# Store queue, rounding order and gated additions in a one-core decoder layer on Trainium2

## The chip, the cores and the metric

The kernel runs on one core of a Trainium2 chip. The core has five engines that the trace shows: TensorE (PE, with its weight loads as PEld), VectorE (DVE), ScalarE (ACT), GpSimd (POOL) and SyncE (SP). Each takes the instructions of its own list in order. SP, ACT and POOL can also issue DMA transfers; the trace shows these as SPq, ACTq and POOLq. The metric is the device time of one execution in microseconds (us); less is better.

## What is computed

The reference is one layer of a decoder trunk for two request groups that share weights: a prompt of 1024 tokens and 8 samples of 8 tokens. The kernel treats them as 1088 columns (NT). Cut to what matters here:

```
h = adaLN(RMSNorm(x), c);  P = h @ w_in
A = rwkv7_branch(P);  B = pool_branch(P)
x = x + gt * ((sigmoid(gA) * (A @ w_br_rwkv) + sigmoid(gB) * (B @ w_br_pool)) @ w_out)
h = adaLN(RMSNorm(x), c)
x = x + gt * (square(relu(h @ w_ff1)) @ w_ff2)      # 1024 -> 4096 -> 1024
y = RMSNorm(x)
```

Everything is float32. The change touches only the MLP, that is, the last three lines, and what stands directly around them.

## The kernel before

**Layout.** Features lie on the 128 partitions, tokens along the free dimension. x is eight tiles of 128 x 1088 (`self.xr[m]`), the hidden layer 32 blocks of 128 rows. A float32 product is made as three matmuls of rounded parts: each operand is split into `hi` (ScalarE's copy to the rounded type) and `lo` (VectorE's or GpSimd's difference), and hi*hi, hi*lo and lo*hi are summed in PSUM. For weights that is `halves` (L193 the rounding, L194 the difference, tiles `whi` and `wlo`); for the MLP's input combinations it is `parts` (L1397 the rounding, L1398 the difference).

**Seven products in place of eight.** Both MLP products are done by a 2x2 scheme with seven block products (numbers c = 0 to 6). For ff1 the halves are the two halves of the tokens (HF = 544 columns each) and the two halves of the 1024 input features; a pair j of hidden blocks is one unit, and there are 16 pairs. `norm2(0)` makes combinations 0 and 1 from the first token half. `norm2(1)` makes combination 5 and then, at L1445, combinations 6, 4, 2 and 3, each of four tiles k. A product of one combination with one weight block is 24 matmuls of 272 columns (`product`), into one of three PSUM tiles `pr`.

**Early pairs.** Products 0 and 1 of the first eight pairs (NE = 8) need only the first token half and run while `norm2(1)` is at work. They are ordered two pairs at a time: (0 of j, 0 of j+1, 1 of j, 1 of j+1). Product 1 is added on top of product 0 in the same PSUM tile, after ScalarE has copied product 0 out (`S["u"]`, L1530); when both are in, ScalarE copies the sum out (`S["o"]`, L1532). Both copies are stored to DRAM (`d_u`, L1533 and L1534) and read back later (L1492, L1493). Then all 16 pairs run, the early ones with products 5, 6, 4, 2, 3, the others with 0, 5, 1, 6, 4, 2, 3. VectorE adds and subtracts the products (L1546, L1548, L1553, L1554, L1558, L1566), ScalarE takes relu and square (L1514, L1515).

**Hidden blocks in DRAM.** For pairs 0 to 11 the combinations that ff2 needs are stored to DRAM: `d_ch` from `combos` (L1597, L1599), from L1573 and L1575, and from `apart` (L1584 for the early pairs, whose tile is a result of ScalarE; L1588 and L1589 for pairs 8 to 11, where ScalarE's rounding and VectorE's difference are stored apart). Pairs 12 to 15 are stored whole (`d_hid`, L1561 and L1569).

**ff2.** Three groups of pairs go through the seven products into accumulators ACC (L1699). `whole` then adds these to x with the gate: `a4 - x` (L1750) where needed, and `residual` (L1882 for the prompt columns, L1885 and L1887 for the sample columns). After ff2's sums, `second` runs `ff2_jobs(6)`: eight jobs, one for each block row m of x, in plain form, whose PSUM tiles (`mm`, `w`) are emptied by `residual` (L1882 again, with `hx<-mm,aq,hx`). After them follow the last group and the final norm.

**Order.** Only TensorE's order is the written one (`manual_schedule` for PE). For the other engines and queues a planner chooses at build time which ready instruction comes next on each list, by its own estimate of time, with the written order as priority; a dependency is the only way to hold an instruction back. The written order itself comes from generators that `Pace` interleaves: a `yield lambda: ...` waits until something has been written, a `yield 1500` until the estimated time has passed. `self.done` holds marks such as `("out", m, i)`.

**Lines that the prediction uses.** L1481 is the load of a raw weight block on SP (two slots `wraw`, four `wr`); L1495, L1497, L1498 and L1508 combine raw blocks; L1596 and L1598 are the first operations of `combos`; L1363 and L1364 are loads that ScalarE issues earlier in the program; L1860 stores the output.

## Time and profile before

| | |
|---|---|
| three runs | 1680.22, 1682.35 (median), 1683.54 us |
| profiled execution, its own time | 1684.85 us |
| its span, first to last instruction | 1683.1 us |
| mean granted TensorE clock | 0.982 |
| moved by DMA | 279.41 MB in 129474 packets |
| first product of the early pairs begins | 950.77 us |
| ff2's sums end, `ff2_jobs(6)` begins | about 1563 us |

How to read it: times in rows of the profile are us from the span's start. A row of a timeline gives start, length, engine, source line, operation, and `out<-in` tiles with shapes; x3 means three merged into one row. A bracket at the end gives the idle time of the engine just before the row and the operation that ended it. A row of a wait view reads "who waited <- for whom: us in total, times, longest us"; an SPq row is a wait at the head of SP's DMA queue. Rows for a source line give shortest/median/longest in ns and the first and last start in us.

### The profile page before, as it was taken

The page shows a single profiled execution, that of the slowest core. Times are in us where ns is not written, and L with a number is a line of the kernel's source. Part 1 is how long each engine was busy: PE and PEld are TensorE (multiplying, and loading weights), DVE is VectorE, ACT ScalarE, POOL GpSimd, SP SyncE. Part 2 cuts the span into 40 slices and gives each one's busy share as a digit, 9 for nine tenths or more (in the row PEclk, how much of TensorE's full clock was granted, in tenths as well). Part 3 has the DMA queues.
Part 4 walks back from the last instruction along what each step waited for, and adds up shares of the span by engine and source line. Part 5 has one row for each costly group of instructions (what it writes and reads, how often), then busy time and mean ns, then how long its engine had stood idle before and what let it go on. Part 6 is the DMA issues. An engine that isn't in the chain of part 4 may idle for free. (4 is left out here: it accounts for less than half of the span.)

```text
span 1683.1 us, 35182 instructions
## 1 busy us (share of the span) xinstructions
PE 1615.6 (96%) x14331; PEld 1503.0 (89%) x14331; DVE 1018.9 (61%) x1677; ACT 680.5 (40%) x1270; POOL 356.3 (21%) x392
## 2 busy tenths in 40 slices
PE   6999999999999999999999999899999999999897
PEld 3989878887888789879989999899999999999897
DVE  5686556845674456334546587675755577667746
ACT  4543333344334333412234464444555554323123
POOL 3311110010000000001622324453322131311221
PEclk9999999999998999999999999999999999999999
DMA  9333413232423242375984467666565876573112
GB/s 337 98 115 130 142 54 120 100 103 70 126 91 102 70 145 85 133 282 188 334 288 158 139 205 238 209 228 229 200 205 191 323 233 209 173 268 122 44 44 107
DMA packets 129474, 279.41 MB, mean 166 GB/s; under 512 B 16768, under 2 KB 31104, under 8 KB 129312
## 3 DMA queue, kind: packets, MB, share of 16 engines
q1 hardware_dynamic: 121632, 255.26, 44.7%
q10 hardware_dynamic: 6048, 16.23, 2.9%
q0 software_dynamic: 1632, 5.67, 1.0%
q8 instruction: 113, 1.85, 0.5%
q14 instruction: 49, 0.40, 0.1%
HBM read 198.15 MB, written 78.95 MB: 165 GB/s over the span
## 5 line engine op out<-in xcount | busy, mean ns | idle before, releaser
L170 PE MATMUL mm<-hx,whi 128*128 128x362 f32 (+1 forms) x1920 | 513.2, 349 | 5.7 <-ACT px L583 1.6
L170 PEld LDWEIGHTS mm<-hx,whi 128*128 128x128 f32 x1920 | 338.4, 193 | 42.4 <-issue 19.0
L170 PE MATMUL pr<-mr,whi 128*128 128x272 f32 x1792 | 340.3, 289 | 8.1 <-DVE hx L1566 6.0
L170 PE MATMUL mm<-hx,wlo 128*128 128x362 f32 (+1 forms) x960 | 318.5, 332 | 0.0
L170 PEld LDWEIGHTS pr<-mr,whi 128*128 128x128 f32 x1792 | 282.9, 190 | 12.0 <-issue 11.9
L170 PE MATMUL pr<-mr,wlo 128*128 128x272 f32 x896 | 259.2, 289 | 0.0
L193 ACT ACTIVATE whi<-wraw 128x512 fp32r<-128x512 f32 x201 | 126.3, 629 | 274.0 <-PE mm L170 83.0
L170 PEld LDWEIGHTS mm<-hx,wlo 128*128 128x128 f32 x960 | 185.0, 193 | 0.0
L194 DVE TENSOR_TENSOR wlo<-wraw,whi 128x512 fp32r<-128x512 f32 x146 | 109.1, 748 | 110.7 <-ACT whi L193 110.5
L170 PE MATMUL pr<-hx,whi 128*128 128x272 f32 x896 | 170.4, 289 | 4.1 <-ACT hid L1530 3.3
L170 PEld LDWEIGHTS pr<-mr,wlo 128*128 128x128 f32 x896 | 170.0, 190 | 0.0
L170 PE MATMUL mm<-mr,whi 128*128 128x272 f32 (+4 forms) x736 | 154.3, 304 | 4.1 <-DVE hx L1882 3.6
L170 PEld LDWEIGHTS pr<-hx,whi 128*128 128x128 f32 x896 | 141.5, 190 | 6.4 <-ACT hid L1530 3.7
L194 POOL TENSOR_TENSOR wlo<-wraw,whi 128x512 fp32r<-128x512 f32 x55 | 80.3, 1461 | 287.7 <-ACT whi L193 277.7
L193 ACT ACTIVATE whi<-wr 128x512 fp32r<-128x512 f32 x123 | 76.4, 627 | 143.8 <-PE pr L170 116.6
L170 PEld LDWEIGHTS mm<-mr,whi 128*128 128x128 f32 x736 | 119.8, 189 | 12.1 <-issue 7.8
L170 PE MATMUL pr<-hx,wlo 128*128 128x272 f32 x448 | 129.6, 289 | 0.0
L170 PE MATMUL mm<-mr,wlo 128*128 128x272 f32 (+4 forms) x368 | 110.7, 301 | 0.0
L194 DVE TENSOR_TENSOR wlo<-wr,whi 128x512 fp32r<-128x512 f32 x94 | 72.7, 774 | 31.3 <-ACT whi L193 31.3
L170 PEld LDWEIGHTS pr<-hx,wlo 128*128 128x128 f32 x448 | 85.0, 190 | 0.0
L170 PE MATMUL pr<-t,whi 128*128 128x272 f32 x448 | 84.4, 287 | 0.0
L1699 DVE TENSOR_TENSOR hx<-hx,pr 128x544 f32<-128x544 f32 x68 | 48.7, 716 | 42.4 <-PE pr L170 42.1
(381 smaller groups left out, 2637.3 us busy)
## 6 DMA issues: line engine op xcount, KB each, us to landing
wr<-in_w_ff SPq DMA_DIRECT2D x123, 256.0 KB, 3.4
wraw<-in_w_ff SPq DMA_DIRECT2D x85, 256.0 KB, 3.1
hid<-d_ch SPq DMA_DIRECT2D x72, 272.0 KB, 4.4
wraw<-in_w_in SPq DMA_DIRECT2D x68, 256.0 KB, 3.0
d_ch<-hx SPq DMA_DIRECT2D x52, 272.0 KB, 3.5
hid<-in_w_ada_mlp SPq DMA_DIRECT2D x24, 512.0 KB, 5.7
d_th<-px SPq DMA_DIRECT2D x22, 544.0 KB, 3.0
wt<-d_x SPq DMA_DIRECT2D x20, 544.0 KB, 4.2
```

Source lines behind the costliest of these rows:

```text
L170: return self.nc.tensor.matmul(out, lhsT, rhs, **kw)
L193: nc.scalar.activation(hi, raw, AF.Copy)
L194: (nc.gpsimd if pool else nc.vector).tensor_tensor(lo, raw, hi.bitcast(F32), op=ALU.subtract)
L1699: nc.vector.tensor_tensor(acc, acc, v, op=ALU.add)
```

## The change

There are three edits.

1. **Stores.** The transfers whose data ScalarE itself wrote last are issued from ScalarE's queue in place of SP's: both `d_u` stores, both `d_hid` stores, `apart`'s store for the early pairs (three a pair) and the `hi` store for pairs 8 to 11 (three a pair). The stores of VectorE's and GpSimd's results stay on SP.
2. **Roundings.** In `norm2(1)` combination 4 is written only after pair 5's second early copy, combination 2 only after pair 7's first. So that the planner keeps this order, the four roundings of each take their scale from a column `one`, which ScalarE fills twice: with a column of that copy, which makes it wait, and then with the constant 1. The column is `g2[:, c, 0:1]`, the prompt's scale, whose last use is before.
3. **Gated additions.** `whole` writes one block row m at a time, after job m-1 of `ff2_jobs(6)` has been written. Row m's gate (`gt[:, m, :]`) and a column -1 (`g2[:, m, 0:1]`) are first filled with a column of row m-1 of x (for m = 0 of the last accumulator), then with their values; the subtraction `a4 - x` becomes `x * (-1) + a4` with that column.

`pair_steps` returns its tile table as "S" for edit 2, and `ff2_jobs` marks ("six", m) for edit 3.

```diff
@@ -1392,9 +1392,9 @@
 
         C = {}
 
-        def parts(c, k, src, pool=False):
+        def parts(c, k, src, pool=False, one=1.0):
             hi, lo = C[c, k] = self.pair(self.hx, "hx", 16) if c < 2 else self.pair(p, "t", 4) if c == 3 else MR()
-            nc.scalar.activation(hi, src, AF.Copy)
+            nc.scalar.activation(hi, src, AF.Copy, scale=one)
             (nc.gpsimd if pool else nc.vector).tensor_tensor(lo, src, hi.bitcast(F32), op=ALU.subtract)
 
         def norm2(i):
@@ -1443,13 +1443,20 @@
             if i:
                 self.done.add(("C", 5))
                 for c in (6, 4, 2, 3):
+                    one = 1.0
+                    if c in (4, 2):
+                        j, h = (NE - 3, 1) if c == 4 else (NE - 1, 0)
+                        yield lambda: ("early", j, h) in self.done
+                        one = g2[:, c, 0:1]
+                        nc.scalar.activation(one, early[j]["S"]["o" if h else "u"][:, 0:1], AF.Copy)
+                        nc.scalar.activation(one, self.kc("one0")[:, 0:1], AF.Copy)
                     for k in range(4):
                         b21 = self.xr[k + 4][:, :HF]
                         if c == 6:
                             nc.vector.tensor_tensor(x[k], x[k + 4], x[k], op=ALU.subtract)
                         elif c == 3:
                             nc.vector.tensor_tensor(b21, tw[k], b21, op=ALU.subtract)
-                        parts(c, k, {6: x[k], 4: self.xr[k][:, :HF], 2: x[k + 4], 3: b21}[c])
+                        parts(c, k, {6: x[k], 4: self.xr[k][:, :HF], 2: x[k + 4], 3: b21}[c], one=one)
                     self.done.add(("C", c))
                     yield 1500
             self.done.add(("h2", i))
@@ -1530,11 +1537,13 @@
                             nc.scalar.activation(v2(S["u"]), v, AF.Copy)
                         elif early:
                             nc.scalar.activation(v2(S["o"]), v, AF.Copy)
-                            nc.sync.dma_start(self.d_u[0][j], S["u"])
-                            nc.sync.dma_start(self.d_u[1][j], S["o"])
+                            nc.scalar.dma_start(self.d_u[0][j], S["u"])
+                            nc.scalar.dma_start(self.d_u[1][j], S["o"])
                         else:
                             nc.scalar.activation(v2(S["o"]), v, AF.Relu)
                             nc.scalar.activation(S["o"], S["o"], AF.Square)
+                        if early == 1:
+                            self.done.add(("early", j, c))
                         return
                     ps = self.ps2()
                     yield from product(ps, c, w, True, True)
@@ -1558,7 +1567,7 @@
                         nc.vector.tensor_tensor(v2(o[:, HF:]), v2(S["u"]), v, op=ALU.add)
                         relu2(o[:, HF:])
                         if kept:
-                            nc.sync.dma_start(self.d_hid[j - 4 * NG], o)
+                            nc.scalar.dma_start(self.d_hid[j - 4 * NG], o)
                         else:
                             combos()
                     else:
@@ -1566,7 +1575,7 @@
                         nc.vector.tensor_tensor(v2(o[:, :HF]), v2(S["u1"]), v, op=ALU.subtract)
                         relu2(o[:, :HF])
                         if kept:
-                            nc.sync.dma_start(self.d_hid[4 + j - 4 * NG], o)
+                            nc.scalar.dma_start(self.d_hid[4 + j - 4 * NG], o)
                         else:
                             b21, b22, t2 = o[:, :HF], o[:, HF:], S["u1"]
                             nc.vector.tensor_tensor(t2, b22, S["u"], op=ALU.subtract)
@@ -1581,11 +1590,11 @@
             def apart(c, x, hi):
 
                 if early:
-                    nc.sync.dma_start(self.d_ch[c][j], x)
+                    nc.scalar.dma_start(self.d_ch[c][j], x)
                     return
                 nc.scalar.activation(hi.bitcast(F32R), x, AF.Copy)
                 nc.vector.tensor_tensor(x.bitcast(F32R), x, hi, op=ALU.subtract)
-                nc.sync.dma_start(self.d_ch[c][j], hi)
+                nc.scalar.dma_start(self.d_ch[c][j], hi)
                 nc.sync.dma_start(self.d_cl[c][j], x)
 
             def combos():
@@ -1599,7 +1608,7 @@
                 nc.sync.dma_start(self.d_ch[6][j], b12)
                 apart(0, b11, S.get("h0"))
 
-            return {c: (prep(c), run(c), c, j) for c in range(7)}
+            return {**{c: (prep(c), run(c), c, j) for c in range(7)}, "S": S}
 
         self.nr = 0
         early, steps = [pair_steps(j, 1) for j in range(NE)], []
@@ -1737,19 +1746,22 @@
         def whole():
 
             yield lambda: "sums" in self.done
-            gq = gt
-            nc.vector.tensor_copy(gq[:, 0, 0:1], ACC[3][1][1][:, 0:1])
-            nc.vector.tensor_copy(gq, self.aq[:, 16:24, :])
-            for mp in range(4):
-                (a1, a4), (a2, a3) = ACC[mp]
+            for m in range(8):
+                if m:
+                    yield lambda: ("six", m - 1) in self.done
+                (a1, a4), (a2, a3) = ACC[m // 2]
+                last = self.xr[m - 1] if m else ACC[3][1][1]
+                one, gate = g2[:, m, 0:1], gt[:, m, :]
+                for x in (one, gate[:, 0:1]):
+                    nc.vector.tensor_copy(x, last[:, 0:1])
+                nc.vector.memset(one, -1.0)
+                nc.vector.tensor_copy(gate, self.aq[:, 16 + m, :])
                 for i, s in enumerate(split):
                     c0, n = s.start, s.stop - s.start
-                    for h in range(2):
-                        x = (a1, a3)[h] if i == 0 else (a2, a4)[h]
-                        if h != i:
-                            nc.vector.tensor_tensor(x, a4, x, op=ALU.subtract)
-                        self.residual(self.xr[2 * mp + h], gq[:, 2 * mp + h, :])(c0, n, x)
-                yield 1500
+                    x = (a1, a3)[m % 2] if i == 0 else (a2, a4)[m % 2]
+                    if m % 2 != i:
+                        nc.vector.scalar_tensor_tensor(x, x, one, a4, op0=ALU.mult, op1=ALU.add)
+                    self.residual(self.xr[m], gate)(c0, n, x)
 
         hid = {}
 
@@ -1764,7 +1776,7 @@
         def ff2_jobs(grp):
             xs = lambda: tuple([hid[4 * grp + j][i] for j in range(4)] for i in range(2))
             return [Job([io["w_ff2"][grp, m // 2][:, m % 2 * 512:m % 2 * 512 + 512]],
-                        lambda m=m: self.residual(self.xr[m], self.aq[:, 16 + m, :]), tags=TG, xs=xs) for m in range(8)]
+                        lambda m=m: self.residual(self.xr[m], self.aq[:, 16 + m, :]), tags=TG, after=lambda m=m: self.done.add(("six", m)), xs=xs) for m in range(8)]
 
         U = lambda j: [(j, h) for h in range(len(j.halves))]
         order = []
```

## The prediction

> **What bounds the kernel now.** I read the page's busy shares, then the view of what TensorE (PE) waited for, then windows that count its matmuls, then the timelines of SP, VectorE (DVE) and ScalarE (ACT) at each hole.
>
> ```profile
> PE 1615.6 (96%) x14331; PEld 1503.0 (89%) x14331; DVE 1018.9 (61%) x1677; ACT 680.5 (40%) x1270; POOL 356.3 (21%) x392
> ```
> ```profile
> PE pr L170 <- DVE hx L1566: 6.0, 4, 3.0
> ...
> PE mm L170 <- DVE hx L1882: 3.6, 2, 2.5
> PE pr L170 <- ACT hid L1530: 3.3, 2, 2.7
> PE w L170 <- DVE rs L1885: 2.1, 1, 2.1
> ```
> ```profile
> 975.77:1000.77 25.00, 21.73 (x160) 21.29 (x159) 22.59 (x37) 16.76 (x31) 2.83 (x1) 0.93 0.51 167
> 1000.77:1025.77 25.00, 25.00 (x203) 25.00 (x203) 13.60 (x17) 13.76 (x24) 10.66 (x8) 1.00 0.77 262
> 1050.77:1100.77 50.00, 44.70 (x331) 44.13 (x331) 34.57 (x41) 22.82 (x39) 24.23 (x15) 0.93 0.64 214
> 1113.27:1138.27 25.00, 23.95 (x191) 23.57 (x189) 19.55 (x25) 11.62 (x19) 11.28 (x8) 1.00 0.67 235
> 1200.77:1250.77 50.00, 50.00 (x404) 50.00 (x403) 32.21 (x43) 28.44 (x46) 15.20 (x11) 1.00 0.67 231
> 1574.00:1590.00 16.00, 10.26 (x47) 9.24 (x46) 10.55 (x24) 0.63 (x1) 5.20 (x9) 0.79 0.11 34
> 1590.00:1606.00 16.00, 16.00 (x99) 16.00 (x98) 5.43 (x13) 1.90 (x3) 2.98 (x4) 1.00 0.16 50
> ```
>
> TensorE is the bound: from 951 on only holes in its stream can be won. The window rows (start:end, length, then busy us and count of PE, weight loads, DVE, ACT, POOL, then granted clock, DMA share, GB/s) price them, slow matmuls after a hole included. An undisturbed 25 us holds 203 matmuls, 50 us 404, 16 us of the last part 99.
>
> - early pairs: 160 for 203, so 43/203 x 25 = **5.3 us** lost;
> - stored early pairs: 331 for 404, 73/404 x 50 = **9.0 us**; and 191 for 203 after 1113, **1.5 us**;
> - gated additions: 47 for 99, 52/99 x 16 = **8.4 us**.
>
> Together 24.2 us, the most that this change can win. The waits fit: L1530 is the early copies, L1566 the stored pairs, L1882 and L1885 the gated additions.
>
> **Part A: 60 stores leave SP for ACT.** They are 16 of d_u, 8 of d_hid, 24 + 12 of d_ch. What SP loses:
>
> ```profile
> 1051.31 0.33 SPq L1584 DMA_DIRECT2D d_ch<-hid  x1
> 1052.04 0.33 SPq L1481 DMA_DIRECT2D wraw<-in_w_ff  x1
> ```
> ```profile
> SPq L1584 <- ACT hid L1515: 3.6, 1, 3.6
> ```
> ```profile
> SPq L1584 <- ACT hid L1515: 3.7, 1, 3.7
> ```
> ```profile
> 1047.05 0.68 DVE L194 TENSOR_TENSOR wlo<-wraw,whi 128x512 fp32r<-128x512 f32 x1
> ...
> 1056.04 0.69 DVE L1495 TENSOR_TENSOR wr<-wraw,wr 128x512 f32<-128x512 f32 x1 [2.27 <-DMA wraw<-in_w_ff]
> ...
> 1058.96 0.71 DVE L1566 TENSOR_TENSOR hx<-hx,pr 128x544 f32<-128x544 f32 x1
> ```
> ```profile
> 1059.81 0.48 PE L170 MATMUL pr<-mr,whi 128*128 128x272 f32 x2 [2.97 <-DVE hx L1566]
> ```
>
> SP holds the store of pair j's Square (L1584) at its head for 3.6 us (windows 1048 to 1053), and 3.7 us in the next such place (1082 to 1088). Behind it stands the load of a weight block. The reader of the slot before it ended at 1047.73 (L194), yet the load goes out at 1052.04 and lands in time for DVE's L1495 only at 1056.04, 4.0 us later. DVE works in order, so L1566, which empties the PSUM bank that TensorE wants at 1056.84 (1059.81 - 2.97), starts at 1058.96. Without the store ahead of it the load can go at about 1048 and L1495 at about 1052, 4 us sooner; L1566 was 2.9 us too late, so the hole closes with about 1 us to spare. Late next is the store of a VectorE result (L1597), which stays on SP. I take four fifths of the 9.0 us and half of the 1.5 us, 7.9 us; bounds 0 (the load is held by the next store instead) and 10.5.
>
> What ACT pays:
>
> ```profile
> 815.79 0.66 ACT L1372 ACTIVATE mr<-t 128x544 fp32r<-128x544 f32 x1 [3.19 <-POOL t L1369]
> 815.79 0.33 ACTq L1363 DMA_DIRECT2D t<-d_th  x1
> 816.35 0.64 ACT L1372 ACTIVATE mr<-t 128x544 fp32r<-128x544 f32 x1
> ...
> 1678.36 1.37 ACTq L1860 DMA_DIRECT2D o_y<-hx  x3
> ```
>
> A load issued beside an activation cost nothing: 815.79 to 816.35 is the 0.56 us by which neighbours follow each other anyway. Three stores in a row took 1.37 us, 0.46 each. A moved store mostly stands right behind its producer, so I take 0.45 us (bounds 0 and 0.46): 60 x 0.45 = 27 us over 370 us, in which ACT is under 60% busy (13.76 of 25, 28.44 of 50). It lies in ACT's idle time except in the early pairs, below. Behind a store on ACT stand weight roundings (L193) and the early copies; TensorE waits for both.
>
> The Trainium skill, DMA: Bandwidth & Descriptors, section "Issuing engines are not separate DMA queues" and its rules table, speaks against this part: all issuing queues use the same 16 DMA engines, so spreading transfers saves sequencer issue time only. By that rule alone part A would bring nothing, and the sum would be 7.9 us smaller; the 3.6 us row is a held issue and not bandwidth, so I side with the row.
>
> **Part B: combinations 4 and 2 rounded later.**
>
> ```profile
> 983.00 5.02 ACT L1397 ACTIVATE mr<-hx 128x544 fp32r<-128x544 f32 x9
> ...
> 994.35 0.61 ACT L1532 ACTIVATE hid<-pr 128x544 f32<-128x544 f32 x1
> ...
> 1000.95 0.60 ACT L1530 ACTIVATE hid<-pr 128x544 f32<-128x544 f32 x1
> ```
> ```profile
> 989.10 0.59 PE L170 MATMUL pr<-hx,whi 128*128 128x272 f32 x2 [2.69 <-ACT hid L1530]
> ```
> ```profile
> 963.00:988.00 25.00, 22.84 (x182) 22.40 (x180) 24.81 (x39) 22.02 (x39) 8.68 (x14) 1.00 0.43 142
> ```
> ```profile
> 1014.85 0.72 DVE L1553 TENSOR_TENSOR hid<-hid,pr 128x544 f32<-128x544 f32 x1 [0.84 <-PE pr L170]
> ```
>
> Nine roundings in a row (5.02 us) stand ahead of pair 5's first copy, for which TensorE waits 2.69 us and then runs slow. Eight of the twelve of this kind now come behind pair 5's second copy (994.35) and pair 7's first (1000.95), so at most four are left ahead, 2.2 us. Their eight subtractions leave DVE too, which was 24.81 of 25 us busy. The deadline: the first product with combination 4 ends with L1553 at 1014.85 and lasts 24 matmuls (24/203 x 25 = 2.96 us), so it starts near 1011.9, or 1006.6 if all 5.3 us of holes go. Four roundings (2.2 us) and their subtractions from 995 on end by 1000, themselves sooner by the same holes; combination 2 from 1001.6 ends by 1007 against 1014.9. Both lie inside TensorE's stream. New work: four one-column activations and a column operand for eight scales. No row has these; their nearest bounds are 0 and a full copy's 0.60 us each, 2.4 us at most, and I take 1 us, hidden after 994. Against the gain stand the d_u stores: ACT is 22.02 of 25 us busy here, and some five or six stores at 0.45 us fill the last 3 us. So of the 5.3 us I take 3.5 (bounds 0 and 5.3; below zero only by the slower rival).
>
> **Part C: gated additions row by row.**
>
> ```profile
> 1567.01 2.10 DVE L1882 SCALAR_TENSOR_TENSOR hx<-hx,gt,hx 128x544 f32<-128x544 f32 x3
> ...
> 1569.93 7.54 DVE L1882 SCALAR_TENSOR_TENSOR hx<-hx,gt,hx 128x544 f32<-128x544 f32 x11
> ...
> 1589.25 1.10 DVE L1882 SCALAR_TENSOR_TENSOR hx<-mm,aq,hx 128x364 f32<-128x364 f32 x2 [4.88 <-PE mm L170]
> 1590.26 0.52 DVE L1882 SCALAR_TENSOR_TENSOR hx<-w,aq,hx 128x298 f32<-128x298 f32 x1
> ...
> 1595.20 1.10 DVE L1882 SCALAR_TENSOR_TENSOR hx<-mm,aq,hx 128x364 f32<-128x364 f32 x2 [3.69 <-PE mm L170]
> ```
> ```profile
> L1750 DVE TENSOR_TENSOR hx<-hx,hx x8: 711/716/1699, 1546.0 to 1566.4; 128x544 f32<-128x544 f32 x8
> ```
>
> All 16 additions stand on DVE ahead of the first bank that TensorE needs back. Spread out, a block row costs two additions and one subtraction, now of the same three-operand form, 3 x 0.69 (7.54/11), the sample part 0.2 and four tiny fills at about 0.15: 2.9 us. A block's own emptying is 1.10 + 0.52 + 0.2, and a weight subtraction (0.68) comes every second block: 2.2 us. Sum 5.1 us in a period of 5.95 (1589.25 to 1595.20): it fits, and the bank is emptied first. Seven of the eight subtractions, hidden before 1564, move into this stretch and are in the sum. The new fills have no row: at 0 the period is 4.5 us, at a 0.69 us operation each 7.3, which would be over. A column is far from 544 elements, so 0.15. Of 8.4 us I take 8.0 (bounds 0 and 8.4).
>
> The Trainium skill, SBUF — State Buffer, section "SBUF: two separate sides", says that a VectorE operation with two SBUF inputs and a GpSimd operation reading SBUF shut each other out for the whole instruction. L1750's longest, 1.70 against 0.71, agrees; by it the periods with a GpSimd weight split would grow to about 6.1 us and part C would be worth a microsecond less.
>
> **Sum.** 7.9 + 3.5 + 8.0 = 19.4 us. The planner draws every engine's list anew from the first changed instruction (about 962) on; I take off 3.4 us for small holes of its own, as the present list has (1.5 us after 1113). Net 16 us. The profiled execution took 1684.85 us (span 1683.1 and 1.75 around it), giving 1668.9; the three runs' median lies 2.5 us lower, and from it I get **1666 us**.
>
> **Rivals.**
> 1. The stores bring nothing: the weight load, freed of L1584, is held by L1597 or L1599 behind it, or by its slot. For it: those rows stay on SP. Against: VectorE waited for that load, and L1597 waits for VectorE. B and C remain, 11.5 us: 1671.
> 2. The new list makes holes as large as those that A and B close, say a weight split behind a store. For it: the list now gives C's rounding order a bad place although nothing forces it. Only C: 1674.
> 3. The block rows are too slow for the period (fills at 0.69), and C does not do what it says; DVE at 7.3 us stretches seven periods by 1.35, 9.5 us, as bad as now. A and B, net 8: 1674.
> 4. Slower: **a store holds ACT** until its data land, by a semaphore that the queue must wait for.
>
> ```profile
> d_u<-hid SPq DMA_DIRECT2D x16, 272.0 KB, 3.1
> ```
> ```profile
> L1584 SPq DMA_DIRECT2D d_ch<-hx x16: 319/383/1125, 1018.8 to 1140.7; - x16
> ```
> Two early pairs give ACT four copies at 0.60 us, four weight roundings of about that size, 4.8 us in all, and four stores, in 4 x 2.96 = 11.8 us of matmuls. With a hold h the excess is 4.8 + 4h - 11.8, four times: it begins at h = 1.75 us, eats C's 8 us at 2.25, and costs 22 us at the landing of 3.1. That gives 1682 - 8 + 22 = 1696, more if the later pairs follow. Against it: the longest issue seen is 1.1 us, and ACT's loads above held nothing.
>
> **How the numbers follow.** Forecast 0.56 (own range 1659 to 1673), rival 1 0.14, rival 2 0.13, rival 3 0.06, rival 4 0.11. The low end, 1658, is the median less all 24.2 us. The high end takes in rivals 1 to 3 with a few microseconds and ends at 1681, which leaves out rival 4. A measurement tells 0.2%, 3.4 us, from no change: faster means under 1679. The forecast, rivals 1 and 3 and half of rival 2 are there, 0.82; the rest of 2 and a little of 4 are the same, 0.08; slower 0.10.
>
> **What would show it.** A: no L1584 among SP's waits, L1495 without a wait of over 2 us, and 404 matmuls per 50 us between 1045 and 1095. B: no run of nine L1397, eight of them behind the copies, and no wait for L1530 over 1 us. C: additions alternating with emptied banks, no wait for L1882 over 0.5 us, and 99 matmuls in each 16 us after 1564. Wrong: ACT standing still behind an issue, weight roundings late by more than a product, or new PE waits summing to over 10 us.

## The result and the profile after

| | before | after |
|---|---|---|
| median (22 runs each) | 1682.62 us (1676.90 to 1690.66) | 1681.61 us (1675.28 to 1691.86) |
| ratio after / before | | 0.9996, 95% interval 0.9983 to 1.0010 |
| profiled execution: time, span, clock | 1684.85, 1683.1, 0.982 | 1678.41, 1676.6, 0.986 |

The change makes no difference that can be measured; 1666 us was forecast. To find where the gain went, both traces are cut at the same pieces of work: the first matmul of the early pairs, of the stored early pairs' remaining forty products, of pairs 8 to 15, of ff2's sums and of `ff2_jobs(6)`, whose eight jobs end the last row. The rows are windows (start:end, length, then busy us and count of PE, weight loads, DVE, ACT, POOL, then clock, DMA share, GB/s). Before:

```profile
950.77:1005.69 54.92, 51.65 (x400) 51.21 (x400) 41.23 (x63) 37.06 (x66) 15.44 (x19) 0.97 0.51 168
1005.69:1136.03 130.34, 124.00 (x963) 122.88 (x961) 92.27 (x109) 60.07 (x100) 63.63 (x39) 0.97 0.68 228
1136.03:1308.97 172.94, 172.94 (x1387) 168.99 (x1385) 103.25 (x140) 92.62 (x151) 49.95 (x36) 1.00 0.61 211
1308.97:1563.01 254.04, 252.25 (x2018) 251.19 (x2017) 175.44 (x236) 106.58 (x173) 59.57 (x41) 1.00 0.64 215
1563.01:1619.78 56.77, 50.61 (x291) 49.29 (x290) 31.83 (x64) 6.14 (x10) 14.25 (x19) 0.94 0.13 42
```

After:

```profile
947.33:997.72 50.39, 49.80 (x400) 49.59 (x400) 42.28 (x62) 37.23 (x67) 14.77 (x19) 1.00 0.53 178
997.72:1130.00 132.28, 123.97 (x962) 122.63 (x961) 92.02 (x111) 61.18 (x103) 63.28 (x39) 0.97 0.66 227
1130.00:1302.94 172.94, 172.94 (x1386) 169.00 (x1385) 102.03 (x140) 92.76 (x151) 49.84 (x36) 1.00 0.60 211
1302.94:1565.00 262.06, 253.39 (x2019) 252.51 (x2017) 170.76 (x229) 106.19 (x173) 59.27 (x41) 0.99 0.62 209
1565.00:1613.27 48.27, 47.85 (x291) 47.54 (x290) 40.82 (x101) 6.14 (x10) 14.27 (x19) 1.00 0.14 48
```

The counts agree stage by stage, so lengths can be subtracted: early pairs -4.5 us, stored early pairs **+1.9**, pairs 8 to 15 unchanged, ff2's sums **+8.0**, gated additions -8.5, what follows unchanged (63.3 us in both); -3.1 us in all. The other 3.4 us between the two spans lie ahead of the first early pair, where nothing was changed (950.77 against 947.33). That start lies between 941.8 and 954.4 us in the twenty profiled executions of this study; in the three kernels that were profiled twice it moved by 0.6, 5.7 and 5.6 us between the two. So below a stage is compared with the same stage, and times by their medians and intervals.

What TensorE waited for after the change (us in total, times, longest):

```profile
PE pr L170 <- DVE hx L1575: 6.8, 5, 3.0
...
PE pr L170 <- ACT hx L1706: 6.1, 1, 6.1
```
```profile
PE pr L170 <- ACT hid L1537: 0.6, 1, 0.6
```

The first row is the old wait for L1566 (now L1575) in the stored pairs, 6.0 us before and not gone. The second is new. The third, from the window of the early pairs, is what is left of the 3.3 us for L1530 (now L1537). No row names the gated additions (L1882, now L1894) any more.

**The new wait** in three timelines of the change, around 1310 us. TensorE:

```profile
1315.22 0.82 PE L170 MATMUL pr<-hx,whi 128*128 128x272 f32 x2 [6.14 <-ACT hx L1706]
```

ScalarE, and its queue ACTq:

```profile
1302.56 0.65 ACT L1522 ACTIVATE hx<-hx 128x544 f32<-128x544 f32 x1
1303.11 0.62 ACT L193 ACTIVATE whi<-wr 128x512 fp32r<-128x512 f32 x1
1310.68 0.33 ACTq L1570 DMA_DIRECT2D d_hid<-hx  x1
1311.06 0.66 ACT L1521 ACTIVATE hx<-hx 128x544 f32<-128x544 f32 x1 [7.33 <-DMA wr<-in_w_ff]
...
1314.11 0.33 ACTq L1578 DMA_DIRECT2D d_hid<-hx  x1
1314.54 0.62 ACT L1706 ACTIVATE hx<-pr 128x544 f32<-128x544 f32 x1 [2.14 <-DMA wr<-in_w_ff]
```

SP's queue:

```profile
1304.99 1.08 SPq L1668 DMA_DIRECT2D wr<-in_w_ff  x2
...
1308.56 0.33 SPq L1668 DMA_DIRECT2D wr<-in_w_ff  x1
```

The first store of the last pair's hidden block (L1570) has its data at 1303.21 (1302.56 + 0.65), yet it leaves at 1310.68. ScalarE, free from 1303.73, stands behind it; the bracket names the landing of a weight load that SP issued. The second store (L1578) holds it again until 1314.11, and the copy of ff2's first sums (L1706), for which TensorE has waited since 1309.08, begins only at 1314.54. The weight load has nothing to do with the store's data. The built program's list of transfers shows the link (time of issue from the trace; S1 to S6 stand for its semaphores 1 to 6):

```
issued   queue  line   counts on  waits for               which is                     landed
1304.99  SP     L1668  S1         S1 >= 1264              the load issued at 1299.43   1304.92
1308.56  SP     L1668  S6         S6 >= 1264              the load issued at 1302.81   1308.50
1310.68  ACT    L1570  S1         ACT done, S1 >= 1280    the load issued at 1304.99   1310.61
1314.11  ACT    L1578  S6         ACT done, S6 >= 1280    the load issued at 1308.56   1314.04
```

Every transfer of SP and of ScalarE counts on one of **eight semaphores that both queues share**, in turn in the planner's order, and leaves only when the transfer eight places before it has landed, whichever queue that was on. In the trace of the change none of the 836 transfers behind the first eight left before that landing. SP is here in a burst of loads, each of which leaves within 0.1 us of such a landing, about every 0.7 us. The store joins that row. Of the sixty stores only these two were held: they left 6.95 and 1.71 us after ScalarE's last operation, the other 58 at most 0.03 us after it. The hole accounts for nearly all of the loss: the first 25.9 us of ff2's sums hold 149 matmuls after the change and 211 before, and 62/211 x 25.9 = 7.6 of the 8.0 us. In the kernel before it stood in the same row on SP and left at 1317.13, 0.06 us after its semaphore's earlier load had landed, but there no engine stood behind it.

### The profile page after: what moved, and what is told of

It reads as the page before. It is cut to its first block, busy times and chain, and to the rows that moved or that the text cites. A ratio compares the mean times of both kernels' runs of the same rounds, so it can differ in the third digit from the quotient of the medians.

```text
span 1676.6 us, 35210 instructions
## 1 busy us (share of the span) xinstructions
PE 1606.3 (96%) x14331; PEld 1496.1 (89%) x14331; DVE 1023.2 (61%) x1707; ACT 681.6 (41%) x1274; POOL 354.9 (21%) x392
## 3 DMA queue, kind: packets, MB, share of 16 engines
q8 instruction: 113, 1.85, 0.4%
## 5 line engine op out<-in xcount | busy, mean ns | idle before, releaser
L193 ACT ACTIVATE whi<-wraw 128x512 fp32r<-128x512 f32 x201 | 126.3, 629 | 262.0 <-PE mm L170 80.8
L193 ACT ACTIVATE whi<-wr 128x512 fp32r<-128x512 f32 x123 | 76.5, 627 | 136.9 <-PE pr L170 110.7
L170 PE MATMUL pr<-hx,wlo 128*128 128x272 f32 x448 | 129.4, 289 | 0.0
```

The costliest lines, as they stand in the source:

```text
L170: return self.nc.tensor.matmul(out, lhsT, rhs, **kw)
L193: nc.scalar.activation(hi, raw, AF.Copy)
```

## Experiments

The table lists all kernels; stages in us from one profiled execution each, cut as above; ratios to the kernel before, run on the same chip, with their 95% intervals. Below the second row the medians are of 6 to 12 executions.

| kernel | early | stored | sums | gated | median | ratio |
|---|---|---|---|---|---|---|
| before | 54.9 | 130.3 | 254.0 | 56.8 | | |
| the change | 50.4 | 132.3 | 262.1 | 48.3 | 1681.61 | 0.9996 (0.9983 to 1.0010) |
| change_again | 50.4 | 131.5 | 264.3 | 48.3 | 1682.78 | 0.9989 (0.9965 to 1.0013) |
| a_only | 54.9 | 127.7 | 267.4 | 57.0 | 1692.19 | 1.0039 (1.0023 to 1.0054) |
| b_only | 50.4 | 129.4 | 256.5 | 57.9 | 1679.83 | 0.9964 (0.9946 to 0.9982) |
| c_only | 54.9 | 130.1 | 254.1 | 48.3 | 1675.13 | 0.9939 (0.9923 to 0.9956) |
| b_c | 50.4 | 129.9 | 256.5 | 48.3 | 1671.92 | 0.9926 (0.9899 to 0.9952) |
| b_c_again | 50.4 | 129.0 | 255.1 | 48.3 | 1671.74 | 0.9927 (0.9899 to 0.9955) |
| hid_on_sp | 50.4 | 130.4 | 254.2 | 48.3 | 1672.65 | 0.9924 (0.9902 to 0.9947) |
| last_hid_sp | 50.4 | 130.8 | 254.6 | 48.3 | 1672.40 | 0.9923 (0.9895 to 0.9950) |
| last_hid_pool | 50.4 | 134.2 | 254.3 | 48.3 | 1671.50 | 0.9924 (0.9899 to 0.9948) |
| pool_stores | 50.4 | 134.0 | 255.3 | 48.3 | 1675.95 | 0.9951 (0.9930 to 0.9972) |
| rb_pool | 50.4 | 128.6 | 254.7 | 48.3 | 1667.15 | 0.9892 (0.9862 to 0.9922) |
| slots | 50.4 | 134.8 | 254.8 | 48.3 | 1674.28 | 0.9936 (0.9911 to 0.9960) |
| slots_rb | 50.4 | 142.3 | 256.6 | 48.3 | 1680.47 | 0.9964 (0.9948 to 0.9980) |
| relu_e | 51.0 | 128.8 | 254.2 | 48.3 | 1669.61 | 0.9904 (0.9877 to 0.9931) |
| direct | 50.9 | 127.4 | 257.1 | 48.3 | 1667.55 | 0.9890 (0.9866 to 0.9914) |
| direct_bc | 51.2 | 124.4 | 255.0 | 48.3 | 1664.86 | 0.9880 (0.9856 to 0.9904) |
| direct_bc_again | 51.2 | 122.9 | 253.6 | 48.3 | 1660.61 | 0.9869 (0.9836 to 0.9902) |
| direct_rb | 50.9 | 133.0 | 254.1 | 48.3 | 1672.77 | 0.9926 (0.9899 to 0.9953) |

### The edits one at a time

a_only, b_only and c_only each make one edit of the diff (1, 2 and 3) and leave the other two out. hid_on_sp is the whole change but for the eight `d_hid` stores:

```diff
-                            nc.scalar.dma_start(self.d_hid[j - 4 * NG], o)
+                            nc.sync.dma_start(self.d_hid[j - 4 * NG], o)
...
-                            nc.scalar.dma_start(self.d_hid[4 + j - 4 * NG], o)
+                            nc.sync.dma_start(self.d_hid[4 + j - 4 * NG], o)
```

> Only the third edit (gated additions by block row). Theory 1, each part acts at its own place: the gated additions' hole of 8.4 us goes and nothing before 1540 us changes, so about 1674.5 us, ratio 0.995. Rival, the planner redraws every list and the parts cannot be told apart: new holes elsewhere, ratio 0.998 to 1.000.

> Only the second edit (combinations 4 and 2 rounded behind early copies). Theory 1: the early pairs' window of 25 us holds about 196 matmuls in place of 160 as in the changed kernel, 4.5 us won, about 1678 us, ratio 0.9973. Rival: the early pairs' gain is paid back in the stored pairs behind them (they begin earlier, their loads do not), ratio 0.999 to 1.001.

> Only the first edit (60 stores on ScalarE's queue). Theory 1: the stored pairs stay as they are or lose 2 us, ScalarE is held for some 7 us by the last pair's store of the hidden rows, which costs TensorE 7 to 8 us, so slower, 1688 to 1692 us, ratio 1.004 to 1.006. Rival, the stores by themselves help and the loss in the changed kernel comes from the other edits' new order: ratio 0.995 to 0.999, and no wait of ScalarE over 3 us at the last pair's store.

> The changed kernel with the eight stores of whole hidden rows (d_hid) back on SP, the other 52 on ScalarE. Theory 1: the hole of 6.14 us at the start of ff2's sums goes, 25 us there hold over 195 matmuls in place of 141, 7 us won against the changed kernel, about 1674 us, ratio to before 0.995. Rival, the hole comes from the burst of loads there (16 transfers in 10 us) and not from the store: it stays, ratio 0.999 to 1.000.

Edit 3 alone takes 8.5 us out of the gated additions, edit 2 alone 4.5 us out of the early pairs. Edit 1 alone makes the kernel slower by 0.39%, and the same hole stands in its trace at the same place (L1697 here is the change's L1706):

```profile
1317.32 0.82 PE L170 MATMUL pr<-hx,whi 128*128 128x272 f32 x2 [7.09 <-ACT hx L1697]
```

Its sums are 13.4 us longer than before. The first 25.9 us of them hold 132 matmuls for 211, which is 9.7 us; the rest lies in later holes that are not traced here.

With the eight `d_hid` stores back on SP the sums take 254.2 us, as before the change. So the change is the sum of two gains and one loss in different stages, and the loss belongs to at most eight stores of sixty.

### Which stores, and by what

last_hid_sp puts back only the two of pair 15; last_hid_pool issues the same two from GpSimd's queue, whose transfers count on eight semaphores of their own:

```diff
-                            nc.scalar.dma_start(self.d_hid[j - 4 * NG], o)
+                            (nc.gpsimd if j == 15 else nc.scalar).dma_start(self.d_hid[j - 4 * NG], o)
...
-                            nc.scalar.dma_start(self.d_hid[4 + j - 4 * NG], o)
+                            (nc.gpsimd if j == 15 else nc.scalar).dma_start(self.d_hid[4 + j - 4 * NG], o)
```

> The change with two of its 60 stores put back on SP: the last pair's two halves of the hidden block. Theory 1 (only these two are held, because each waits for a load of the burst that SP issues at that time): TensorE's wait of 6.14 us for the first sums' copy is gone, the stretch of the second weight's sums falls from 262 to 254 us, and the ratio is that of the run with all eight put back, 0.992. Theory 2 (each of the eight costs ScalarE something, or all 60 do): half of the 8 us or more stays, a ratio of 0.995 or above.

> The change with the last pair's two stores of the hidden block on GpSimd's queue, whose transfers count on semaphores that SP's and ScalarE's do not use. Theory L (the store was held because its semaphore was that of the transfer eight places before in the shared count of SP and ScalarE, a load of the burst): the store leaves within 1 us of the activation that makes its data, in the midst of the same burst, and the second weight's sums take 254 to 256 us. Rival (a store cannot be issued into the burst, whatever its semaphore, since the transfers before it fill the queues): it leaves 5 us or more after its data are ready.

> Edits 2 and 3 alone: all 60 stores of ScalarE's results stay on SP's queue. Theory 1 (the two edits add up, and edit 1 is worth nothing in the stored pairs): 4.5 us gained over the sixteen early products and 8.5 us over the gated additions, 13 us below the kernel before, a ratio of 0.992; the forty stored products take 130 us, as they did before, and the start of the second weight's sums shows no wait of TensorE over 2 us. Theory 2 (the stores on ScalarE's queue were worth something beside the last pair, which the time with only those eight put back then includes): the stored products take 132 us or more here, and the time lies 2 us or more above that of the run with the eight put back.

The two stores are the whole loss: 254.6 us and a ratio of 0.9923 with these alone on SP. GpSimd's and ScalarE's timelines of last_hid_pool tell the mechanism:

```profile
1302.67 0.58 POOL L1570 DMA_DIRECT2D d_hid<-hx  x1 [10.44 <-DVE t L1656]
1304.90 0.55 POOL L1578 DMA_DIRECT2D d_hid<-hx  x1 [1.65 <-ACT hx L1522]
```
```profile
1301.73 0.64 ACT L1522 ACTIVATE hx<-hx 128x544 f32<-128x544 f32 x1
...
1303.94 0.66 ACT L1522 ACTIVATE hx<-hx 128x544 f32<-128x544 f32 x1
```

Each store leaves 0.30 us after the activation that makes its data (1302.37 and 1304.60), in the midst of the same burst, in which the DMA engines are busy throughout. So a store can be issued into the burst. GpSimd's queue differs from ScalarE's in more than the semaphores (an issue takes 0.55 to 0.58 us here, 0.33 on ScalarE's); that it was the shared semaphore which held the store on ScalarE rests on this run together with the list of waits above and the 0.07 us between the landing there and the store. b_c, the change without edit 1, is as fast as the kernels that keep 52 or 58 of the stores on ScalarE's queue: these are worth nothing that can be measured.

### Why the stored early pairs do not get shorter

SP no longer waits for ScalarE's stores, as the prediction wanted. What SP's queue waited for in the forty stored products, before and then after:

```profile
SPq L1597 <- DVE hid L1596: 21.0, 7, 7.2
SPq L1584 <- ACT hid L1515: 16.3, 7, 3.7
SPq L1481 <- DVE wr L1497: 13.3, 6, 4.1
SPq L1481 <- POOL wraw L1508: 11.6, 6, 3.5
```
```profile
SPq L1488 <- DVE wr L1504: 27.1, 7, 6.8
SPq L1606 <- DVE hid L1605: 24.8, 7, 6.5
SPq L1488 <- POOL wraw L1515: 17.9, 5, 5.6
```

The 16.3 us are gone. But the load (L1481, now L1488) waits 45.0 us in place of 24.9 for its place, that is, for the combination (L1497 and L1508, now L1504 and L1515) that reads the block there before, and VectorE's store (L1597, now L1606) waits 24.8 in place of 21.0. VectorE's L1495 (now L1502) waits for loads as long as ever: 16.9 and 3.5 us before, 21.2 after. The timelines of the change at its largest hole show the circle; VectorE, ScalarE, GpSimd, then SP:

```profile
1064.12 0.69 DVE L1502 TENSOR_TENSOR wr<-wraw,wr 128x512 f32<-128x512 f32 x1 [5.76 <-DMA wraw<-in_w_ff]
...
1065.45 1.65 DVE L1504 TENSOR_TENSOR wr<-wr,wr 128x512 f32<-128x512 f32 x1
1067.03 1.78 DVE L1605 TENSOR_TENSOR hid<-hx,hid 128x544 f32<-128x544 f32 x1
1068.73 0.71 DVE L1575 TENSOR_TENSOR hx<-hx,pr 128x544 f32<-128x544 f32 x1
```
```profile
1060.50 0.66 ACT L1521 ACTIVATE hid<-hid 128x544 f32<-128x544 f32 x1 [5.28 <-DMA hid<-d_u]
```
```profile
1059.24 1.29 POOL L1515 TENSOR_TENSOR wraw<-wraw,wr 128x512 f32<-128x512 f32 x1 [3.94 <-DMA wraw<-in_w_ff]
```
```profile
1056.03 0.46 SPq L1500 DMA_DIRECT2D hid<-d_u  x1
1060.55 0.33 SPq L1488 DMA_DIRECT2D wr<-in_w_ff  x1
1060.98 0.38 SPq L1488 DMA_DIRECT2D wraw<-in_w_ff  x1
```

L1575, for which TensorE waits, stands behind L1502; L1502 waits for the load of 1060.98; that load stands behind the one that leaves at 1060.55, when L1515 has freed a place (1059.24 + 1.29 = 1060.53); and L1515 waited for an earlier load. At the same time ScalarE stands 5.28 us for a read-back that SP issued at 1056.03. Four kernels try these waits, singly and together, all with the eight `d_hid` stores on SP. pool_stores issues the stores of VectorE's and GpSimd's results (`d_ch[3]` to `d_ch[6]`) from GpSimd's queue; rb_pool the read-back; slots gives the loads more places; slots_rb is slots and rb_pool together. The cuts are from pool_stores, rb_pool and slots, in this order:

```diff
-                            nc.sync.dma_start(self.d_ch[5][j], t2)
+                            nc.gpsimd.dma_start(self.d_ch[5][j], t2)
...
-                            nc.sync.dma_start(S["u"], self.d_u[0][j])
-                            nc.sync.dma_start(S["o"], self.d_u[1][j])
+                            nc.gpsimd.dma_start(S["u"], self.d_u[0][j])
+                            nc.gpsimd.dma_start(S["o"], self.d_u[1][j])
...
+                if early == 2 and self.nr % 5 in (2, 4):
+                    t = D[key] = HX(F32)[:, :512]
+                else:
+                    q, tag, bufs = (self.wp, "wraw", 2) if self.nr % (5 if early == 2 else 3) == 0 else (p, "wr2", 4)
```

> The change with the eight stores of hidden blocks on SP, and the stores of VectorE's and GpSimd's combinations of the stored early pairs moved from SP's to GpSimd's queue, so that SP holds loads alone there. Theory 1a (the weight load is held by the store of a VectorE result at the head of SP's queue): SP's waits for the subtraction are gone, and the forty stored products fall from 130.4 us towards 122, a ratio near 0.987. Theory 1b (it is held by its slot: SP then waits for the slot as long as it waited for the store): they take 129 us or more, and the ratio stays at 0.992 within 0.002. Should the stores hold GpSimd, whose weight split feeds TensorE, the forty products take more than 132 us.

> The change with the eight stores of hidden blocks on SP, and the read-back of the early pairs' first sums issued from GpSimd's queue in place of SP's. Theory 1c (ScalarE's activation waits 4 to 6 us for a read-back that SP issues late, and that wait is what holds the period): the forty stored products fall from 130.4 us by 3 us or more. Theory 1b (the slots of the raw weight hold it): 129 us or more, no change in the time against the run with the eight put back.

> The eight hidden-block stores on SP, and in the stored early pairs two raw weight blocks of five take a row of the sixteen hx rows, so that a block's place is free again after ten blocks and not after six. Theory 1b (the load of the weight waits for its place, wr of the VectorE subtraction or wraw of the GpSimd one): SP's waits for these two, 46 us in the forty stored products, go below 15 us, and the forty products fall from 130.4 us to 126 or less. Theory 1a (the store of a VectorE result at SP's head holds the loads whatever the places): SP's wait for the subtraction L1605 (25 us before) grows and the forty products take 129 us or more. Theory 1d (engine order holds it: ScalarE, VectorE and TensorE wait for each other's results in turn): both waits of SP fall and the forty products still take 129 us or more.

> As the run with more places, and the read-back issued from GpSimd's queue as well. Theory 1b with 1c (places and read-back each hold a part): 124 us or less for the forty stored products, against 128.6 with the read-back alone moved, and a ratio near 0.986. If the places hold nothing: 128 to 129 us and a ratio of 0.989.

pool_stores: SP's waits in its forty stored products name L1606 no more, but the loads get nothing from it:

```profile
SPq L1488 <- DVE wr L1504: 36.2, 6, 6.5
SPq L1499 <- DMA d_ch<-hid: 18.5, 4, 9.2
```

SP now waits longer for the place, and for a tile whose store, late on GpSimd's queue, had not landed. The stage took 134.0 us and the ratio was 0.9951, which is theory 1b's sign in the stage but outside its range for the ratio. The stage is also over the 132 us named for a held GpSimd: that engine stood 13.2 us for the data of these stores, though no wait of TensorE names it, and VectorE was busy 99.8 us, against 92.0 in hid_on_sp. So this run shows that taking the store from SP's head is not enough, and not more. slots did not settle the places. SP's waits for L1504 and L1515 (L1507 and L1518 there) fell from 46.0 to 27.4 us, not below the 15 that theory 1b needs, and that for the store from 25.5 to 13.7, yet the stage took 134.8 us: of the three theories only 1d, the engines' order, has these signs. But the other dealing of the places also brought SP a wait of 37.9 us for weight splits on VectorE, so the test isn't clean. slots_rb, 142.3 us, was worse than either expectation. rb_pool came between its two: 1.8 us shorter in the stage, and a ratio whose interval overlaps that of hid_on_sp.

The row of ScalarE gave a new theory (R). L1521 there takes relu of `S["o"]`, the sum of products 0 and 1 of an early pair. It needs only the read-back, so the planner puts it as early as it believes the data to be there: the store behind it at 1062.28 is that of pair 6, while the stores around it are of pair 3. ScalarE stands in order for a block that is wanted three pairs later, with weight copies (L193) behind. relu_e takes relu and square before the block is stored, so that none are left behind the read-back; direct also stores it straight to `d_ch[0]`, where the combination went anyway, and reads it back from there. Both keep the eight `d_hid` stores on SP. The cut is from direct:

```diff
                         elif early:
-                            nc.scalar.activation(v2(S["o"]), v, AF.Copy)
+                            nc.scalar.activation(v2(S["o"]), v, AF.Relu)
+                            nc.scalar.activation(S["o"], S["o"], AF.Square)
                             nc.scalar.dma_start(self.d_u[0][j], S["u"])
-                            nc.scalar.dma_start(self.d_u[1][j], S["o"])
+                            nc.scalar.dma_start(self.d_ch[0][j], S["o"])
...
-                        if early:
-                            relu2(S["o"])
...
-                apart(0, b11, S.get("h0"))
+                if not early:
+                    apart(0, b11, S.get("h0"))
```

direct_bc is direct without edit 1, every one of these stores on SP; direct_rb is direct with rb_pool's read-back.

> The eight hidden-block stores on SP, and relu and square of the early pairs' second sums done before they are stored, straight into the place of the combination, so that a stored pair has neither the two activations nor that store left. Theory R (ScalarE stood 22 us in five waits, in its own order, for a read-back that was needed three pairs later, and its weight copies behind it): these waits are gone, the forty stored products fall from 130.4 us to 125 or less, the sixteen early products grow by 1 us at most (50.4 before), and the ratio is 0.989 or less. Theory 1b (the loads' places hold the period whatever ScalarE does): 128 us or more, and ScalarE waits for loads or for VectorE in their place.

> As direct, but the block is still stored to the scratch place and read back, and its combination is stored again from ScalarE's queue behind the read-back. Theory R with the store counted: the store now waits for the read-back's landing at the head of ScalarE's queue as the activation did, so that half of the gain of direct or more is lost (the forty products take 127 us or more). If the activations alone held ScalarE: 125 us or less, as direct.

> As direct, with the stores of ScalarE's results that are left all back on SP's queue, as before the change. If the stores on ScalarE's queue are worth what was forecast once ScalarE no longer waits for the read-back: the forty products take 4 us or more longer than in direct. If they are worth nothing there either: within 2 us of direct.

> As direct, with the read-back issued from GpSimd's queue. Theory R: the read-back is no longer waited for early, and the forty products stay within 2 us of direct. Otherwise (the read-back held more than ScalarE's order): 2 us or more below direct.

ScalarE's waits in the forty stored products, of b_c_again, of relu_e and of direct_bc:

```profile
ACT hid L1521 <- DMA hid<-d_u: 12.3, 4, 5.0
ACT hid L1521 <- DMA wr<-in_w_ff: 10.6, 2, 6.0
```
```profile
ACT hx L1521 <- DMA hid<-d_u: 27.9, 5, 7.2
```
```profile
ACT hx L1521 <- DVE hx L1574: 36.2, 7, 5.7
ACT whi L193 <- PE pr L170: 17.0, 19, 2.4
```

In relu_e the store behind the read-back takes over the wait, as expected (128.8 us). In direct and direct_bc no wait for a read-back (`hid<-d_u`) is left. direct met the expected ratio, but its stage, 127.4 us, did not reach 125: VectorE's L1502 still waits 27.4 us for loads. direct_bc did (124.4 us); it was expected within 2 us of direct or longer and came out 3.0 us shorter. So the stores on ScalarE's queue gain nothing here either. direct_rb, 5.6 us above direct, missed its expectation, and why is open; GpSimd's own work stands behind the read-back there, and VectorE was busy 98.9 us in its stage, against 91.2 in direct.

direct and direct_bc change more than ScalarE's wait: they also save one store of 272 KB for each of the eight pairs. relu_e, which keeps that store, stayed inside the spread of the kernels without early squares (given below). And in direct_bc L1504 took 0.69 us on average, against 1.08 and 0.96 in b_c's two traces, which is 2 to 3 us over its eight. So the early square with its direct store shortens the stage; how much of that is ScalarE's wait was not separated.

### How far one profile can be trusted

> The change once more, unaltered. If the first edit cost what the runs so far say: the hole of TensorE at the start of the second weight's sums is there again (6 us or more, that stretch 262 us), the forty stored products take 130 us or more, and the ratio lies between 0.998 and 1.002. If either was an accident of the first execution: a stretch of 254 to 257 us, or forty products in 126 us or less.

> Edits 2 and 3 alone once more, unaltered. Forty stored products in 129 to 131 us and a ratio of 0.992 if the four runs without the stores on ScalarE's queue (130.3, 130.1, 129.4, 129.9 us) were typical; outside 128 to 132 us if they agreed by chance.

> Edits 2 and 3 with relu and square before the store, once more, unaltered. If that storing is worth what the first execution showed: forty products in 126 us or less, and a time 4 us or more below edits 2 and 3 alone on the same chip. If not: 128 us or more, and the same time within 2 us.

All three repeat. Five executions with SP's stores as before the change and nothing else altered in the stage (before, b_only, c_only, b_c twice) take 129.0 to 130.3 us there, mean 129.7. Six with the early pairs' stores on ScalarE's queue (the change twice, a_only, hid_on_sp, last_hid_sp, last_hid_pool) take 127.7 to 134.2, mean 131.1. So no gain of edit 1 shows there, and a difference of 2 us between two such executions means nothing. direct_bc with 124.4 and 122.9 lies outside the spread. On one chip the change took 11.0 us more than b_c (1682.78 against 1671.74; 9.2 us in the sums and 2.6 in the stored pairs of those two traces). direct_bc took another 11.1 less, of which its stage shows 6.1 and the sums 1.5, with 0.8 lost in the early pairs, 6.8 us in all. The start of the early pairs was 6.2 us earlier in its trace, but nothing ahead of it was touched, so the rest of the 11.1 us stays open. In both comparisons it has the lowest ratio of the study, 1.2% and 1.3% under the kernel before.

## Why the prediction was wrong, point by point

- **Part A, the gain (7.9 us taken, bounds 0 and 10.5): about 0, the lower bound.** The step that failed is "Without the store ahead of it the load can go at about 1048 and L1495 at about 1052, 4 us sooner". In that one hole the row of L1495 itself left less: VectorE was idle only 2.27 us for the load. Ahead of that it stood for a rounding of ScalarE, and ScalarE, whose Square the store waited for, stood for a read-back. These rows of the kernel before show it; the bracket of L1514 names a weight load, but its own input is the read-back issued at 1045.30, which landed at 1049.78:

```profile
1053.08 0.69 DVE L194 TENSOR_TENSOR wlo<-wr,whi 128x512 fp32r<-128x512 f32 x1 [4.44 <-ACT whi L193]
```
```profile
1045.30 0.79 SPq L1493 DMA_DIRECT2D hid<-d_u  x1
```
```profile
1049.94 0.66 ACT L1514 ACTIVATE hid<-hid 128x544 f32<-128x544 f32 x1 [4.44 <-DMA wr<-in_w_ff]
```
  So in this order of VectorE's list the load alone could have brought L1495 forward by 2.3 us at most, less than the 2.97 us of the hole. Over the whole stage the load already waited 24.9 us for L1497 and L1508, a view that I had not read; with the store gone these waits grew by 20.1 us, more than the 16.3 us that left. This is rival 1, to which I gave 0.14; that the place decides rather than the next store is how the waits read, and no run shows it. What closed part of the holes was the early square with its direct store, which takes ScalarE's wait for the read-back away, and not a wait that edit 1 touches. What bounds the remaining 123 to 124 us (960 matmuls at the 0.124 us of pairs 8 to 15, 172.94/1387, would be 120) stays open, since the test of the places was not clean.
- **Part A, ScalarE's cost (27 us, "in ACT's idle time except in the early pairs"): right in size, wrong in what it put at nothing.** From a store to ScalarE's next row it was 0.50 us in the median of the sixty, against the 0.45 taken. The early pairs take 54.9 us in a_only as in before, and 50.4 us with or without the stores: they cost nothing there. The second step that failed is the hold itself, which the sum put at nothing. "A semaphore that the queue must wait for" was the right mechanism of the slower rival, but I put it in the early pairs and took the store's own landing, 3.1 us. It is the landing of somebody else's transfer, and it struck two stores of sixty, where SP is in a burst and TensorE waits for ScalarE at once; it cost 8.0 us, in the second execution 10.2. "ACT's loads held nothing" was no evidence: for the load shown, at 815.79, the transfer eight places ahead had landed 10.6 us before.
- **Part B (3.5 us taken): 4.5.** Right. Four roundings are left ahead of the copy; combinations 4 and 2 come as runs of four behind their columns, and cost more than a plain copy. These rows of the change show it, beside the earlier run of nine (5.02 us together, each row 0.64 us long):

```profile
987.40 0.20 ACT L1451 ACTIVATE g<-hid 128x1 f32<-128x1 f32 x1 [0.40 <-ACT hid L1539]
...
987.87 2.68 ACT L1397 ACTIVATE mr<-hx,g 128x544 fp32r<-128x544 f32 x4
```
  Four columns at 0.20 us and eight roundings at 0.09 us more (each row 0.74 us long against 0.64) are 1.5 us, inside my bounds of 0 and 2.4, hidden as said. The share that I left out for the `d_u` stores was not needed.
- **Part C (8.0 us taken, upper bound 8.4): 8.5.** Right, and the period fits. One period of the change on VectorE, the bank emptied first:

```profile
1576.80 1.10 DVE L1894 SCALAR_TENSOR_TENSOR hx<-mm,aq,hx 128x364 f32<-128x364 f32 x2 [1.24 <-PE mm L170]
...
1578.51 1.19 DVE L1758 COPY gt<-aq 128x9 f32<-128x9 f32 x1
...
1579.62 0.92 DVE L1763 SCALAR_TENSOR_TENSOR hx<-hx,g,hx 128x544 f32<-128x544 f32 x1
...
1582.75 1.10 DVE L1894 SCALAR_TENSOR_TENSOR hx<-mm,aq,hx 128x364 f32<-128x364 f32 x2 [0.75 <-PE mm L170]
```
  VectorE is idle 0.75 us of the 5.95 here: 5.2 us of work, 5.1 forecast. That the two agree so closely is partly luck: this period has a fill of 1.19 us in place of 0.15 and no weight subtraction of VectorE, and the periods that have one leave 1.24 us idle.
- **The planner's own holes (3.4 us off):** b_c's sums are 1.0 to 2.5 us longer than before and its forty stored products 0.5 to 1.4 shorter. This allowance was not what failed.
- **The two cited rules.** The Trainium skill, DMA: Bandwidth & Descriptors, "Issuing engines are not separate DMA queues", says that another issuing queue saves only sequencer time; by it part A brings nothing, and that is what the stored pairs show (131.1 us against 129.7). The 8.0 us lost in ff2's sums are a held issue, which that rule is not about. By the Trainium skill, SBUF — State Buffer, "SBUF: two separate sides", periods with a GpSimd weight split were to grow to about 6.1 us. Such a delay shows: the fill of nine columns took 1.03 to 1.19 us where that split ran and 0.17 elsewhere. But the period stayed at 5.95, with 0.75 us of VectorE's idle time still left.

Rivals 1 and 4 came true together, one in each stage. I had priced them as alternatives; with B and C at 13.0 us, no gain from A and its loss of 8.0, their sum is 5.0 us under the time before, and the stored pairs' +1.9 brings it to 3.1. In the second execution the same sum (10.2 lost in the sums, 1.2 in the stored pairs) leaves 1.6; the medians differ by 1.0.

## What to carry to other kernels

A store moved to a compute engine's queue cost that engine half a microsecond here, unless the semaphore it counts on still belonged to a transfer in flight, of whichever queue. Look for the place where another queue is in a burst and something critical follows the store, and price the landing of the transfer ahead in that count, not of the store itself. Before crediting a wait removed from the head of a queue, sum every wait of the transfer behind it over the whole stage: the next one may be as long. And look on an in-order engine for work that needs only a transfer and is placed far ahead of its use.

## What was not expected of the hardware

VectorE's two-operand work of these shapes took 0.69 to 0.72 us alone and up to 1.8 us beside a GpSimd operation: L1504 and L1605 in the circle above took 1.65 and 1.78 us, 2.0 us more than alone, of the 3.0 us by which L1575 came late. Which instruction is hit changes with the phase: L1504 took 0.69 us on average in direct_bc's forty products and 1.85 in pool_stores'. That may be why kernels with the same work there differ by some us; it was not tested.
